# Moving the first half's merged low parts from GpSimd to VectorE, spacing out the second half's gate loads, and one scaling and one store of the last rows

## The chip, the cores and the metric

One core of one Trainium2 chip runs the whole program. The metric is the device time of one execution in microseconds (us); the kernel before takes 1205.59 us (median of 3 runs, 1204.64 to 1205.98). Smaller is better. Engines: TensorE (PE) multiplies matrices, and loads of its weights have a row of their own, PEld; VectorE (DVE), ScalarE (ACT) and GpSimd (POOL) do elementwise work; SyncE (SP) issues nearly all DMAs. Each engine runs its own list of instructions strictly in order; semaphores tie the lists together.

## The reference

1024 tokens of width 1024 with 16 meta tokens ahead of them go through one mixer block, one squared-ReLU MLP and a final RMS norm. The part that matters here is the merge at the end of the mixer:

```python
y_b = jnp.einsum('blc,cd->bld', o.reshape(B, L, GLA_VAL), w_gla_out)
m = jax.nn.sigmoid(ga) * y_a + jax.nn.sigmoid(gb) * y_b
return jnp.einsum('bld,de->ble', m, w_out)
```

`o` is the gated linear attention output (4 heads of 128 values), `y_a` the output of the pooling branch. After the MLP each row is divided by its root mean square and multiplied by `norm_final`.

## The kernel before, in words

**Arithmetic.** Products are float32 of near full precision: every operand is split into a high part (a rounding copy by ScalarE) and a low part (operand minus high part), and TensorE adds three products, high by high, high by low and low by high (`mm3`, L256 to L258). So each intermediate that is multiplied again costs one ScalarE copy and one subtraction, on VectorE or GpSimd.

**The merge.** Tokens are handled in two halves `h` of 512. All tensors are transposed, channels on partitions. The merged tensor `m` has 8 channel blocks `d` of 128 for each half. `yb_block(n, h)` (L1127) makes two of them: TensorE multiplies 256 columns of `w_gla_out` (a high and a low slot of the ring `W1`) by the attention output `yg[h]`, heads k = 0 to 3 in this order, 12 matmuls for each block; VectorE multiplies the PSUM bank by the stored gate sigmoid(gb) (buffer `gl`: L1161 for h = 0, L1150 for h = 1), and adds the stored sigmoid(ga)·y_a (buffer `ml`, L1162); ScalarE makes the high part `th` (L1165); the low part `tl` is then GpSimd's for h = 0, in two instructions of 256 columns (L1169), and VectorE's for h = 1, where it is put off until after the next block's gate product (`pending`, `late()`, L1167). I call the blocks first-half 0 to 7 and second-half 0 to 7.

**Buffers and loads.** Gates and stored products come from DRAM, 256 KB each, issued by SP: `yb_load` (L1086) writes the first half's into `t1` and `o`, the second half's into `t2` and `o2`, each a ring of three buffers. A buffer can be loaded again when its last reader is done: for `gl` that is the low part. `early_gates` (L1104), called after the last attention unit's inner part has been written down, opens `t2` and `o2`, asks for a piece of `w_out`, and asks for the second half's first three pairs at once. It also opens a section in which the instructions of ScalarE and VectorE stand in the order of the code; elsewhere a scheduler orders them. TensorE's are in the order of the code throughout.

**What runs at the same time.** The first half's blocks fill TensorE's gaps in the last attention unit, p = 1 of the second half (`across`, L1339): the chunk states (L1367), the two parts of the output (L1376 and L1386), its norm (L1395 to L1400), a transpose (L1404), and the gating that writes `yg` for heads 2 and 3 (L1413, L1411 on VectorE, high parts L1415 on ScalarE, low parts L1418 on VectorE). L1381 on ScalarE copies one column of the output bank; L1386 on TensorE waits for it. In the same stretch the ring `W1` is refilled: ScalarE makes the high part of a slot (L83), GpSimd the low part in four pieces until the attention is done (`W1.eng = pool`), VectorE after that (L87).

Behind the second half's blocks stands `out_tile`, which multiplies `m` by `w_out`. The split of `w_out` comes in four pieces kk, 256 rows each (L1498 on ScalarE, L1499 on VectorE); pieces 1 to 3 are loaded (L1490) into `acc`, which lies where `t1`, `o` and other buffers of the attention were, so the load of piece 1 waits until the last reader of those is done. SP stands in the order of the code from there on, and the second half's later gate loads are behind that load on SP.

**The end.** The last 4 row tiles t = 0 to 3 (`finish_row` with tail, L1729) leave one after the other: VectorE adds the last product (L1767), ScalarE squares and sums the left half (L1742), the inverse root takes two ScalarE steps (L220, L222) and four small VectorE ones (L221, L224, L228, L229), ScalarE scales the right half (L1745), VectorE the left half (L1746), and SP stores first the right half, then the left half (L1748).

Of the kernel before, what the change touches and what calls it, by code (L numbers as in the profile page):

```python
# [11 lines left out]
ACT = mybir.ActivationFunctionType  # L12
ALU = mybir.AluOpType
AX = mybir.AxisListType

P = 128
# [4 lines left out]
HALF = 512  # L21
# [93 lines left out]
def kernel(  # L115
# [3 lines left out]
    nc = tc.nc  # L119
    x = x[0]  # L120
    out = out[0]
# [4 lines left out]
    act, dve, pool, pe = nc.scalar, nc.vector, nc.gpsimd, nc.tensor  # L126
# [74 lines left out]
    def f32(ap):  # L201
        return ap.bitcast(F32)
# [256 lines left out]
    def nxt(key):  # L459
        i = S["n" + key]  # L460
        S["n" + key] += 1
        return S[key][:, i % S["d" + key]]
# [625 lines left out]
    def yb_load(n, h):  # L1088

        if n >= 8 or (n, h) in staged:  # L1090
            return
        d = 2 * YB[h][n // 2] + n % 2
        gl, ml = staged[n, h] = (nxt("t2"), nxt("o2")) if h else (nxt("t1"), nxt("o"))
        nc.sync.dma_start(gl, gb_dram[d, h])
        nc.sync.dma_start(ml, ma_dram[d, h])
# [10 lines left out]
    def early_gates():  # L1106

        in_order("order", mybir.EngineType.Activation, mybir.EngineType.DVE)
        left.pop_to(S["left_n"])
        for key in ("t2", "o2"):  # L1110
            S[key] = right.push(key, [P, 3, HALF], F32)
            S["n" + key], S["d" + key] = 0, 3
        S["raw3"] = right.push("raw3", [P, D], F32)
        fetch_wo(0, 0, S["raw3"])
        for n in range(3):
            yb_load(n, 1)

    kept, pending = {}, []

    def late():  # L1120

        while pending:
            pending.pop(0)()

    halves_of_half = [slice(k * HALF // 2, (k + 1) * HALF // 2) for k in range(2)]

    def yb_block(n, h):  # L1127
        j = YB[h][n]

        def fn(*wbs):  # L1130
            if h == 0 and n > 1:
                kept[j] = wbs[0]
            wb = wbs[0] if wbs else kept[j]
            hi, lo = (t.rearrange("p (k c) -> p k c", k=4) for t in wb)
            assert h or ("o", 0) in done
            yg = S["yg"][h]
            for e in range(2):
                d, w = 2 * j + e, slice(e * P, (e + 1) * P)
                for m in range(2):
                    yb_load(2 * n + e + m, h)  # L1140
                gl, ml = staged[2 * n + e, h]
                b = bank("mm")
                for k in range(4):
                    mm3(
                        b, 1, lambda i: (hi[:, k, w], lo[:, k, w]),
                        lambda i: (yg[:, 0, k], yg[:, 1, k]), first=k == 0, last=k == 3,
                    )
                    yield 3 * 512 / 2400
                if h:
                    dve.tensor_tensor(gl, b, gl, ALU.mult)  # L1150
                    late()
                    yb_load(2 * n + e + 2, h)
                if e and not wbs:
                    W1.done, W1.kept = W1.done + 1, W1.kept - 1
                    W1.top_up()
                elif e:
                    yield "keep" if j in kept else "free"
                if h and e and n == 1:
                    load_wo(0, 1)()
                if not h:  # L1160
                    dve.tensor_tensor(gl, b, gl, ALU.mult)  # L1161
                dve.tensor_tensor(gl, gl, ml, ALU.add)  # L1162
                th = MH[h][:, d]
                tl = ML[h][:, d]
                act.activation(th, gl, ACT.Copy)  # L1165
                if h:
                    pending.append(lambda tl=tl, gl=gl, th=th: dve.tensor_tensor(tl, gl, f32(th), ALU.subtract))  # L1167
                for c in halves_of_half[: 2 - 2 * h]:
                    pool.tensor_tensor(tl[:, c], gl[:, c], f32(th[:, c]), ALU.subtract)  # L1169

        return fn

# [557 lines left out]
    def finish_row(t, tail):  # L1730

        a, (h0, h1) = S["c"][:, t], halves()
        junk = S["w2"]["12"].rearrange("p i c -> p (i c)")[:, (t % 4) * D : (t % 4 + 1) * D]
        if not tail:
            ss = ln_stat[t % 4]
            act.activation(junk, a, ACT.Square, accum_out=ss)
            rs = inv_sqrt(ss, 1, 1.0 / D)
            dve.scalar_tensor_tensor(junk, a, rs, gB, ALU.mult, ALU.mult)
            nc.sync.dma_start(out[t * P : (t + 1) * P, :], junk)
            return  # L1740
        s0, s1 = tails[t]
        act.activation(junk[:, h0], a[:, h0], ACT.Square, accum_out=s0)  # L1742
        dve.tensor_scalar(s1, s1, 1.0 / D, EPS, ALU.mult, ALU.add)
        rs = inv_sqrt(s0, 1, 1.0 / D, s1)
        act.activation(junk[:, h1], a[:, h1], ACT.Copy, scale=rs)  # L1745
        dve.scalar_tensor_tensor(junk[:, h0], a[:, h0], rs, gB[:, h0], ALU.mult, ALU.mult)  # L1746
        for c in (h1, h0):
            nc.sync.dma_start(out[t * P : (t + 1) * P, c], junk[:, c])  # L1748

    tails = [(tiny(1), tiny(1)) for _ in range(4)]  # L1750

# [126 lines left out]
```

## Time and profile before

| what | us |
|---|---|
| median of 3 runs | 1205.59 |
| the profiled execution | 1206.74 |
| its span, first to last instruction | 1205.0 |
| around the span (1206.74 - 1205.0) | 1.7 |
| PE busy | 1186.7 |
| DVE busy | 874.9 |
| ACT busy | 623.9 |
| POOL busy | 60.2 |

The profile is of one execution. A line of the timeline tells the start, the duration, the engine, the source line, the operation with the names out<-in, and, in brackets, how long the engine had been idle and what ended that. A row "x4" merges four equal instructions and runs from the first one's start to the last one's end. In the names, `t` is a gate buffer (`t1` or `t2`), `o` a buffer of stored products, `th` and `tl` the merged tensor's high and low parts, `mix` the attention's scratch, `raw` a weight as loaded, `w1h` and `w1l` the ring's slots. Granted clock is TensorE's share of full speed; it is 0.998 over this span.

### The profile page before, as it was taken

To read this page: it belongs to the slowest core of one execution; us is meant where nothing else is said; L and a number is where in the kernel's file an instruction comes from. 1 tells how busy PE (TensorE), PEld (TensorE's weight loads), DVE (VectorE), ACT (ScalarE), POOL (GpSimd) and SP (SyncE) were. 2 spreads that over 40 slices of the span, in tenths; PEclk is the share of its full clock that TensorE was granted. 3 is DMA by queue.
4 is the path that set the end of the run, shared out by engine and by line. 5 is a ranking of instruction groups with operands and counts; after the bars stand their busy time and mean duration, and the time that the engine had idled before them with its cause. 6 is when DMAs were issued, how large, how long until landed. Compare 5 with 4: busy or idle time off the path is not lost.

```text
span 1205.0 us, 18370 instructions
## 1 busy us (share of the span) xinstructions
PE 1186.7 (98%) x6794; PEld 992.4 (82%) x6794; DVE 874.9 (73%) x1438; ACT 623.9 (52%) x1119; POOL 60.2 (5%) x98
## 2 busy tenths in 40 slices
PE   7999999999999999999999999999999999999997
PEld 7878888898998887888878888888888888888885
DVE  7997677667567887637886767667675887887685
ACT  7677566755446433315654545455454444445554
POOL 2000000000103235000000000000000000000000
PEclk9999999999999999999999999999999999999999
DMA  9043333445107675922254445444479963333532
GB/s 258 2 114 114 109 103 104 150 120 150 64 20 260 188 252 187 324 74 83 88 181 151 158 134 171 143 164 154 135 263 334 338 224 98 97 97 94 169 97 88
DMA packets 144555, 182.24 MB, mean 151 GB/s; under 512 B 10265, under 2 KB 81713, under 8 KB 143953
## 3 DMA queue, kind: packets, MB, share of 16 engines
q1 hardware_dynamic: 143856, 176.81, 46.0%
q0 software_dynamic: 608, 4.26, 1.0%
q8 instruction: 53, 0.87, 0.3%
q14 instruction: 38, 0.30, 0.1%
HBM read 123.36 MB, written 57.67 MB: 150 GB/s over the span
## 4 chain that ended last, share of the span: by engine, by line
PE 89%; DVE 5%; ACT 2%; DMA 2%; issue 1%; POOL 0%; SPq 0%; DVEq 0%; POOLq 0%; ACTq 0%
PE b_mm L256 10%; PE b_mm L258 10%; PE b_mm L257 10%; PE b_ms L258 10%; PE b_ms L257 10%; PE b_ms L256 10%; PE b_x L257 8%; PE b_x L256 8%; PE b_x L258 8%; PE b_sc L1253 1%; PE b_mx L256 1%; DMA ma_dram<-o 1%; PE b_mx L258 1%; PE b_mx L257 1%; DVE ut L787 1%
## 5 line engine op out<-in xcount | busy, mean ns | idle before, releaser
L256 PE MATMUL b_mm<-th,w1h 128*128 128x512 f32 (+1 forms) x308 | 115.5, 375 | 1.5 <-DVE c L822 1.0
L258 PE MATMUL b_mm<-th,w1l 128*128 128x512 f32 (+1 forms) x308 | 114.2, 371 | 0.0
L257 PE MATMUL b_mm<-tl,w1h 128*128 128x512 f32 (+1 forms) x308 | 114.1, 371 | 0.0
L256 PE MATMUL b_x<-th,w1h 128*128 128x512 f32 (+1 forms) x264 | 100.2, 379 | 0.0
L257 PE MATMUL b_x<-tl,w1h 128*128 128x512 f32 (+1 forms) x264 | 100.1, 379 | 0.0
L258 PE MATMUL b_x<-th,w1l 128*128 128x512 f32 (+1 forms) x264 | 99.7, 378 | 0.0
L274 ACT ACTIVATE w1h<-raw 128x512 fp32r<-128x512 f32 x98 | 60.7, 620 | 28.1 <-PE b_ms L257 13.6
L274 ACT ACTIVATE w1h<-fs 128x512 fp32r<-128x512 f32 x78 | 49.0, 630 | 47.9 <-PE b_ms L257 33.7
L275 DVE TENSOR_TENSOR w1l<-raw,w1h 128x512 fp32r<-128x512 f32 x98 | 67.0, 685 | 8.0 <-ACT w1h L274 8.0
L256 PEld LDWEIGHTS b_mm<-th,w1h 128*128 128x128 f32 x308 | 57.8, 188 | 12.4 <-issue 1.4
L258 PEld LDWEIGHTS b_mm<-th,w1l 128*128 128x128 f32 x308 | 57.8, 188 | 10.1
L257 PEld LDWEIGHTS b_mm<-tl,w1h 128*128 128x128 f32 x308 | 57.9, 188 | 9.6
L275 DVE TENSOR_TENSOR w1l<-fs,w1h 128x512 fp32r<-128x512 f32 x78 | 53.4, 686 | 16.2 <-ACT w1h L274 16.1
L274 ACT ACTIVATE w1h<-bt 128x512 fp32r<-128x512 f32 x44 | 27.8, 632 | 67.1 <-issue 62.7
L258 PEld LDWEIGHTS b_x<-th,w1l 128*128 128x128 f32 x264 | 49.7, 188 | 9.5
L256 PEld LDWEIGHTS b_x<-th,w1h 128*128 128x128 f32 x264 | 49.6, 188 | 9.4
L257 PEld LDWEIGHTS b_x<-tl,w1h 128*128 128x128 f32 x264 | 49.6, 188 | 9.3
L1726 DVE TENSOR_TENSOR bt<-w,w 128x512 f32<-128x512 f32 x80 | 54.7, 684 | 2.0 <-DMA w<-in_w_ff_dram 2.0
L274 ACT ACTIVATE fxh<-bt 128x512 fp32r<-128x512 f32 x36 | 22.8, 632 | 55.7 <-issue 50.1
L274 ACT ACTIVATE w1h<-rawx 128x512 fp32r<-128x512 f32 x44 | 27.5, 628 | 44.8 <-PE b_x L257 18.7
L258 PE MATMUL b_ms<-wo,w1l 128*128 128x512 f32 x128 | 49.9, 390 | 0.0
L256 PE MATMUL b_ms<-wo,w1h 128*128 128x512 f32 x128 | 49.8, 389 | 0.0
(452 smaller groups left out, 3331.8 us busy)
## 6 DMA issues: line engine op xcount, KB each, us to landing
hf_dram<-h SPq DMA_DIRECT2D x112, 256.0 KB, 2.1
raw<-hf_dram SPq DMA_DIRECT2D x112, 256.0 KB, 2.7
w<-in_w_ff_dram SPq DMA_DIRECT2D x64, 256.0 KB, 4.6
raw<-in_w_in_dram SPq DMA_DIRECT2D x22, 512.0 KB, 4.4
raw<-in_w_ff_dram SPq DMA_DIRECT2D x16, 512.0 KB, 4.1
rawx<-in_w_ff_dram SPq DMA_DIRECT2D x16, 512.0 KB, 4.1
rawx<-in_w_in_dram SPq DMA_DIRECT2D x10, 512.0 KB, 4.2
xs<-in_x_dram SPq DMA_DIRECT2D x8, 512.0 KB, 5.6
```

The source lines that it names most:

```text
L256: pe.matmul(ps, ah, bh, start=first and i == 0, stop=False, skip_group_check=more)
L257: pe.matmul(ps, ah, bl, start=False, stop=False, skip_group_check=more)
L258: pe.matmul(ps, al, bh, start=False, stop=last and i == n - 1, skip_group_check=more)
L274: act.activation(hi, a, ACT.Copy)
L275: dve.tensor_tensor(lo, a, f32(hi), ALU.subtract)
L787: dve.tensor_tensor(to_, a_, b_, ALU.subtract)
L1253: pe.matmul(b[to, e, j], kk[r, s], qq[r, s], start=True, stop=True, tile_position=(e * CH, u * CH))
L1726: dve.tensor_tensor(bt, w, S["w2"][q[3:]][:, i], ALU.add if q[2] == "+" else ALU.subtract)
```

## The change

Three edits that do not depend on each other:

- First half: the low part leaves GpSimd's two instructions of 256 columns and becomes one VectorE instruction of 512 columns, right behind the high part in the code. The second half's still waits for the next block.
- `early_gates` asks for one pair of the second half instead of three. The second and third pair are asked for in the first half's `yb_block` of n = 2 and n = 3, in the second of its two blocks.
- Last rows: the scaling of the right half of row tile 2 goes from ScalarE to GpSimd; the right half of row tile 3 is stored by ScalarE instead of SP.

```diff
-        for n in range(3):
-            yb_load(n, 1)
+        yb_load(0, 1)
...
-    halves_of_half = [slice(k * HALF // 2, (k + 1) * HALF // 2) for k in range(2)]
...
                 if h and e and n == 1:
                     load_wo(0, 1)()
+                if e and not h and n > 1:
+                    yb_load(n - 1, 1)
                 if not h:
                     dve.tensor_tensor(gl, b, gl, ALU.mult)
                 dve.tensor_tensor(gl, gl, ml, ALU.add)
                 th = MH[h][:, d]
                 tl = ML[h][:, d]
                 act.activation(th, gl, ACT.Copy)
+                low = lambda tl=tl, gl=gl, th=th: dve.tensor_tensor(tl, gl, f32(th), ALU.subtract)
                 if h:
-                    pending.append(lambda tl=tl, gl=gl, th=th: dve.tensor_tensor(tl, gl, f32(th), ALU.subtract))
-                for c in halves_of_half[: 2 - 2 * h]:
-                    pool.tensor_tensor(tl[:, c], gl[:, c], f32(th[:, c]), ALU.subtract)
+                    pending.append(low)
+                else:
+                    low()
...
-        act.activation(junk[:, h1], a[:, h1], ACT.Copy, scale=rs)
+        if t == 2:
+            pool.tensor_scalar(junk[:, h1], a[:, h1], rs, None, ALU.mult)
+        else:
+            act.activation(junk[:, h1], a[:, h1], ACT.Copy, scale=rs)
         dve.scalar_tensor_tensor(junk[:, h0], a[:, h0], rs, gB[:, h0], ALU.mult, ALU.mult)
-        for c in (h1, h0):
-            nc.sync.dma_start(out[t * P : (t + 1) * P, c], junk[:, c])
+        for q, c in ((act if t == 3 else nc.sync, h1), (nc.sync, h0)):
+            q.dma_start(out[t * P : (t + 1) * P, c], junk[:, c])
```

The lists of instructions that this gives stand against the old ones as follows. TensorE's is the same, instruction for instruction. In the changed kernel the lines of `yb_block` are L1147 (gate product, second half), L1160 (gate product, first half), L1161 (sum), L1164 (high part) and L1165 (low part); `t_2694` is `t1`, `t_4590` is `t2`.

VectorE before, from the first half's blocks 4 and 5 to the first two of the second half; the attention's last gating (L1413, L1411, L1418) stands behind block 5:

```order
L1161 TENSOR_TENSOR t_2694<-b_mm,t_2694 128x512
L1162 TENSOR_TENSOR t_2694<-t_2694,o 128x512
L1413 TENSOR_TENSOR mix<-b_m_4816,mix 128x512
L1411 TENSOR_TENSOR mix<-b_m_4816,mix 128x4x64 x2
L1418 TENSOR_TENSOR yg_3485<-mix,yg_3485 128x512 x2
L1161 TENSOR_TENSOR t_2694<-b_mx,t_2694 128x512
L1162 TENSOR_TENSOR t_2694<-t_2694,o 128x512
L1161 TENSOR_TENSOR t_2694<-b_mm,t_2694 128x512
L1162 TENSOR_TENSOR t_2694<-t_2694,o 128x512
L1150 TENSOR_TENSOR t_4590<-b_mm,t_4590 128x512
```

VectorE now, from block 5's product to the low part of block 6 and, behind the rows shown as "...", that of block 7:

```order
L1160 TENSOR_TENSOR t_2694<-b_mm,t_2694 128x512
L1161 TENSOR_TENSOR t_2694<-t_2694,o 128x512
L1165 TENSOR_TENSOR tl_136<-t_2694,th_132 128x512
L1413 TENSOR_TENSOR mix<-b_m_4808,mix 128x512
L1411 TENSOR_TENSOR mix<-b_m_4808,mix 128x4x64 x2
L1418 TENSOR_TENSOR yg_3485<-mix,yg_3485 128x512 x2
...
L1165 TENSOR_TENSOR tl_136<-t_2694,th_132 128x512
...
L87 TENSOR_TENSOR w1l<-raw_120,w1h 128x1024
L1165 TENSOR_TENSOR tl_136<-t_2694,th_132 128x512
```

Each first-half block has gained a row, L1165, behind its sum: it reads `th`, which ScalarE writes from that sum, and the next block's product stands behind it. The low parts of blocks 3, 4 and 5 now stand ahead of the attention's gating, that of block 7 behind the refill of a `W1` slot (L87).

SyncE (all DMAs), in the stretch where the first half's blocks 2 and 3 ask for their gates; `raw_116` is one of the two buffers in which `w_gla_out` arrives. One piece of the difference:

```order
 L1095 DMA o<-ma_dram 128x512
+L1094 DMA t_4590<-gb_dram 128x512
+L110 DMA raw_116<-in_w_gla_out_dram 128x4x256
+L963 DMA ma_dram<-o 128x512
+L1094 DMA t_2694<-gb_dram 128x512
+L1095 DMA o<-ma_dram 128x512
+L1094 DMA t_2694<-gb_dram 128x512
+L1095 DMA o<-ma_dram 128x512
+L1393 DMA mix<-r_dram 128x2x512
 L1094 DMA t_4590<-gb_dram 128x512 x2
-L963 DMA ma_dram<-o 128x512
-L1094 DMA t_4590<-gb_dram 128x512
```

The weight load of 512 KB now stands ahead of the last store of the pooling branch (L963), two gate loads of the second half behind it.

## The prediction

> **What bounds the kernel now.** I read the page first, engine shares and chain, then the timeline of the stretch that the change touches.
>
> ```profile
> PE 1186.7 (98%) x6794; PEld 992.4 (82%) x6794; DVE 874.9 (73%) x1438; ACT 623.9 (52%) x1119; POOL 60.2 (5%) x98
> PE 89%; DVE 5%; ACT 2%; DMA 2%; issue 1%; POOL 0%; SPq 0%; DVEq 0%; POOLq 0%; ACTq 0%
> ```
>
> TensorE is busy 98% of the span and carries 89% of the chain. Its list of instructions stays the same, so the time moves only where TensorE's waits change, or behind its last product. In the merge the timeline shows two waits:
>
> ```profile
> 455.95 0.45 PE L1386 MATMUL b_m<-W,mix 64*64 64x128 f32 x8 [1.18 <-ACT small L1381]
> 462.92 0.47 PE L256 MATMUL b_mx<-yg,w1h 128*128 128x512 f32 x1 [0.20 <-DVE t L1161]
> ```
>
> Together 1.38 us: all that the two edits of the merge can win. What they can lose is set by VectorE's room there, from the windows (PE, PEld, DVE, ACT, POOL busy):
>
> ```profile
> 469.37:491.10 21.73, 21.73 (x97) 18.02 (x96) 20.69 (x27) 8.22 (x11) 5.80 (x5) 1.00 0.57 180
> ```
>
> In the second half's eight blocks VectorE is busy 20.69 of 21.73 us, beside a TensorE without a gap. Work put on VectorE ahead of this stretch has nowhere to go.
>
> **First wait: L1386.** The chain of waits (start, duration, what) that leads to it:
>
> ```profile
> 444.80 6.78 DMA ma_dram<-o
> 451.64 2.74 DMA o<-ma_dram
> 454.48 0.70 DVE t L1162
> 455.20 0.63 ACT th L1165
> ```
>
> The last store of the pooling branch lands at 451.58, the products of first-half block 2 are loaded into its buffer, the sum and the high part follow, and L1381, behind that high part on ScalarE, lets L1386 go. Now SP has the weight load (512 KB) ahead of that store, and it waits until GpSimd has read its buffer:
>
> ```profile
> 442.37 3.00 POOL L87 TENSOR_TENSOR w1l<-raw,w1h 128x256 fp32r<-128x256 f32 x4 [10.82 <-ACT w1h L83]
> 448.00:450.00 2.00, 2.00 (x11) 1.61 (x10) 1.86 (x6) 0.93 (x1) 1.08 (x3) 1.00 1.02 386
> ```
>
> GpSimd ends at 445.37, so the store is issued near 445.9 instead of 444.80, 1.1 us later, and has 512 KB ahead of it where a 256 KB gate load stood.
> At the 386 GB/s of the second row (last column) 256 KB more are 0.7 us. If both add up, +1.8 us. In the other direction the two gate loads that no longer compete can let it land earlier; then VectorE sets the end: it now has block 1's low part ahead of block 2, which I place at 452.5 to 453.2, so block 2's sum can start at 453.95, 0.5 us before the 454.48 above. The queue is full either way, so issuing later costs little of itself; I take **+0.4 us**, bounds -0.5 and +1.8.
>
> **The low parts' round trips.** Block by block, VectorE before, from block 3 on to the attention's gating (L1413, L1411, L1418):
>
> ```profile
> 462.09 0.68 DVE L1161 TENSOR_TENSOR t<-b_mx,t 128x512 f32<-128x512 f32 x1
> 462.81 1.25 DVE L1162 TENSOR_TENSOR t<-t,o 128x512 f32<-128x512 f32 x1
> 467.15 0.68 DVE L1413 TENSOR_TENSOR mix<-b_m,mix 128x512 f32<-128x512 f32 x1
> 467.75 0.74 DVE L1411 TENSOR_TENSOR mix<-b_m,mix 128x256 f32<-128x256 f32 x2
> 468.53 2.39 DVE L1418 TENSOR_TENSOR yg<-mix,yg 128x512 fp32r<-128x512 f32 x2
> 461.39 3.27 POOL L87 TENSOR_TENSOR w1l<-raw,w1h 128x256 fp32r<-128x256 f32 x4 [4.07 <-ACT w1h L83]
> 464.80 5.57 POOL L1169 TENSOR_TENSOR tl<-t,th 128x256 fp32r<-128x256 f32 x6
> ```
>
> Blocks 3, 4 and 5 take 467.15 - 462.09 = 5.06 us. Now each has its low part behind the sum, it needs ScalarE's high part, and VectorE, strictly in order, waits for that. The second half shows one such trip:
>
> ```profile
> 479.39 0.68 DVE L1162 TENSOR_TENSOR t<-t,o 128x512 f32<-128x512 f32 x1
> 480.11 0.63 ACT L1165 ACTIVATE th<-t 128x512 fp32r<-128x512 f32 x1 [2.00 <-DVE t L1162]
> 480.78 0.69 DVE L1167 TENSOR_TENSOR tl<-t,th 128x512 fp32r<-128x512 f32 x1
> 481.38 0.69 DVE L1162 TENSOR_TENSOR t<-t,o 128x512 f32<-128x512 f32 x1
> ```
>
> From the sum's end (480.07) to the low part's start 0.71, to the next instruction 0.60 (481.38 - 480.78). A block is 0.72 (462.09 to 462.81) + 0.68 + 0.71 + 0.60 = 2.71 us; block 3, whose sum still runs beside GpSimd's refill, has 1.25 for 0.68, 3.28. Three blocks: 8.70, +3.64, so L1413 starts at 470.79. I use 0.68 for the sums of 4 and 5, since GpSimd's 16 halves are gone.
>
> The Trainium skill, "SBUF — State Buffer", section "Who interferes with whom", says that a VectorE instruction with two SBUF inputs and a GpSimd instruction that reads SBUF exclude each other, the second waiting until the first is done. The rows agree: the sum took 1.25 beside GpSimd's refill and 0.68 at 479.39 with GpSimd idle; if the stretch had another cause and stayed, blocks 4 and 5 would be 0.57 longer each, +1.1 us on the sum.
>
> Behind L1413 the gating takes its turns with ScalarE, two high parts in 1.29, the second after L1411: high part of head 2 at 471.51 to 472.14, of head 3 at 472.16 to 472.79; low part of head 2 472.18 to 472.87, of head 3 472.83 to 473.52. TensorE before:
>
> ```profile
> 469.37 0.39 PE L256 MATMUL b_mm<-yg,w1h 128*128 128x512 f32 x1
> 470.95 0.39 PE L257 MATMUL b_mm<-yg,w1h 128*128 128x512 f32 x1
> 472.08 0.39 PE L256 MATMUL b_x<-yg,w1h 128*128 128x512 f32 x1
> ```
>
> The second half's block 0 starts at 469.37, nothing holds it there (first-half block 5's bank is read by 468.8), and at 470.95 it multiplies head 2's low part. That comes at 472.87; TensorE starts 0.15 behind a release (462.77 to 462.92 above): 473.02, a wait of **+2.1 us**. Head 3's follows 0.68 later and is on time. Bounds 1.5 (trips 0.2 shorter each) and 2.6 (GpSimd's refill slows one more).
>
> **SP, behind block 7's low part.** The load of `w_out` piece 1 goes where `t1` lay. It waited for GpSimd's last half; now it waits for block 7's low part on VectorE:
>
> ```profile
> 477.82 0.38 SPq L1490 DMA_DIRECT2D acc<-in_w_out_dram x1
> 478.37 0.35 SPq L1094 DMA_DIRECT2D t<-gb_dram x1
> DMA to landing us min/median/max: 4.3/4.3/4.3
> 482.74 0.69 DVE L1150 TENSOR_TENSOR t<-b_mm,t 128x512 f32<-128x512 f32 x1 [0.67 <-DMA t<-gb_dram]
> 483.95 1.22 DVE L87 TENSOR_TENSOR w1l<-raw,w1h 128x1024 fp32r<-128x1024 f32 x1
> 486.14 0.39 PE L258 MATMUL b_x<-yg,w1l 128*128 128x512 f32 x1
> ```
>
> VectorE's list from head 3's low part (next start 473.43) to block 7's: nine instructions of 512 columns at 0.60, two of 1024 at about 1.13 (1.22 less the overlap of 0.09 that the 0.69 to 0.60 above shows), and 0.3 until second-half block 0 ends on TensorE: 473.43 + 5.40 + 2.26 + 0.3 = 481.4, done 482.1. So this load goes out 4.3 us later, though TensorE is only 2.1 later, and what is queued behind it on SP goes with it: the gate of second-half block 3, 0.55 behind, lands 4.3 after that, 487.0. VectorE already waited 0.67 for it; now its product starts at 487.1, and behind it stand a low part and L87, the low part of the weights of second-half block 6: 488.3 to 489.5. TensorE wants them at 486.14 + 2.1 = 488.2 and gets them at 489.65: **+1.4 us**. Bounds 0 (the gate lands in 2.9) and 2.2.
>
> Last of this kind is `w_out` piece 3:
>
> ```profile
> 493.54 1.22 DVE L1499 TENSOR_TENSOR wo<-acc,wo 128x1024 fp32r<-128x1024 f32 x1
> 495.43 0.39 PE L257 MATMUL b_mm<-wo,th 128*128 128x512 f32 x1
> ```
>
> From 488.3 on stand three more instructions of 1024 columns and nine of 512 ahead of it, 8.8 us: 497.1 to 498.3, with up to 0.5 for a gate. TensorE wants it at 495.43 + 2.1 + 1.4 = 498.9. On time: **0**, at most +0.8. What follows on TensorE moves with it: its list is the same, and its few waits behind it hang on its own results.
>
> **The last rows.** ScalarE's scaling of row 2 stands inside row 3's chain:
>
> ```profile
> 1198.36 0.71 ACT L1745 ACTIVATE w<-c,small 128x512 f32<-128x512 f32 x1
> 1198.97 0.28 ACT L220 ACTIVATE small<-small 128x1 f32<-128x1 f32 x1
> 1200.90 0.33 SPq L1748 DMA_DIRECT2D out_dram<-w  x1
> 1201.35 0.36 SPq L1748 DMA_DIRECT2D out_dram<-w  x1
> DMA to landing us min/median/max: 2.5/2.5/2.5
> 249.46 1.29 POOL L877 TENSOR_TENSOR mw<-raw,mw 128x512 fp32r<-128x512 f32 x1 [9.00 <-DMA gb_dram<-o]
> ```
>
> Without it L220 can start up to 0.61 earlier, less the end of the squaring ahead of it: 0.4. The trace has no GpSimd instruction of this kind; L877 with two inputs takes 1.29, and with one input it should not take longer. It runs beside VectorE's scaling of row 2, and if that stretches by 0.57 (1.25 against 0.68 above), the 0.4 is gone. The last store no longer waits behind its neighbour on SP: 1201.35 - 1200.90 = 0.45. No ScalarE store is in the trace: at best it also lands as the first of a pair does (another 0.4), at worst the new queue costs as much as a slow landing does against the 2.5 here (4.3 - 2.5 = 1.8). I take -0.45 and half of the 0.4: **-0.6 us**, bounds -1.2 and +1.0.
>
> The Trainium skill, "DMA: Bandwidth & Descriptors", section "Issuing engines are not separate DMA queues", says that an issue from another engine saves only the time of the issue, since all share the 16 DMA engines. By that the gain is the 0.45; if the queues were independent, 0.85. No run here shows it yet.
>
> **Sum.** 0.4 + 2.1 + 1.4 + 0 - 0.6 = +3.3 us. On the profiled execution, 1205.0 span and 1.7 around it, 1206.74 + 3.3 = 1210.0; that execution is 1.15 above the median of the runs, so on the median 1205.59 + 3.3 = **1208.9 us**.
>
> **Rivals.**
>
> *The round trip alone.* SP's delay is absorbed, because the gate lands 1.4 us faster into idle DMA queues. For it: nothing else is under way there. Against: the row above had idle queues too, and took 4.3. Sum 0.4 + 2.1 - 0.6 = +1.9: 1207.5.
>
> *The queue ahead of L1386 grows.* The store lands the full 1.8 later. For it: SP's blocked load; against: the full DMA queue. Sum 1.8 + 2.1 + 1.4 - 0.6 = +4.7: 1210.3.
>
> *VectorE is free in time.* The other side: the gating keeps its place, both waits go, and the tail wins. The gating is on time if the three blocks take at most 8.70 - 2.1 = 6.6 us, 0.7 less for each, which is just the wait for ScalarE; this would need the scheduler's order not to hold on VectorE. For it: GpSimd's reads did stretch VectorE, the pair L1418 took 2.39 where two times 0.68 would do. Against: I have already counted that, and the low part stands behind the sum in the list. Sum -1.38 - 0.6 = -2.0: 1203.6.
>
> **How the numbers follow.** The forecast 0.58, its own range 1208.0 to 1209.9; the round trip alone 0.20; the longer queue 0.14; the free VectorE 0.08. About 0.2% (2.4 us) is what a measurement of this kernel can tell from no change. Slower: 0.58 + 0.14, less 0.02 for forecasts that end below 1208.0: 0.70. Within: 0.20 + 0.02 + 0.05 of the free VectorE: 0.27. Faster: 0.03, since even -2.0 falls short. The range goes from 1206.8 (the round trip alone with the lower bound 1.5 of the trips) to 1211.2 (the longer queue with 0.9 more from refill or tail).
>
> **What would show it.** Right: TensorE waits about 2 us at L257 of second-half block 0 for VectorE's L1418, and over 1 us at an L258 near 489 for L87; L1490 goes out near 482; L1386 waits 1 to 2 us; the last store is issued before 1201 plus the delay so far. Wrong: no wait at L1418 (the round trips are not paid), L1490 near 478 (block 7's low part is early), or a new wait behind 500, which I have taken for none.

## The result, and the profile after

| what | before | changed |
|---|---|---|
| median (6 executions each, taken side by side), us | 1205.78 (1204.64 to 1207.00) | 1212.39 (1211.98 to 1213.17) |
| ratio to before | | 1.0056, 95% interval 1.0045 to 1.0067 |
| the profiled execution, us | 1206.74 | 1212.29 |
| its span, us | 1205.0 | 1210.5 |
| end of TensorE's last product, us | 1196.97 | 1201.52 |
| from there to the end of the span, us | 7.99 | 9.00 |

The changed kernel is 6.6 us slower; 3.3 were forecast, and 1211.2 was the end of the range. Of the 5.5 us between the two profiled spans, 4.55 lie ahead of TensorE's last product and 1.0 behind it. Another 1.0 is the choice of the execution: the profiled one of before lies 0.96 above its median, the changed one 0.10 below.

In the page after, the shares (first row) and the chain (second row) read nearly as before; TensorE's waits are too short to show there.

```profile
PE 1189.9 (98%) x6794; PEld 994.6 (82%) x6794; DVE 876.6 (72%) x1446; ACT 623.3 (51%) x1118; POOL 48.1 (4%) x83
PE 87%; DVE 6%; ACT 2%; DMA 2%; issue 1%; POOL 0%; SPq 0%; DVEq 0%; POOLq 0%; ACTq 0%
```

VectorE has eight instructions more and only 1.7 us more of busy time: GpSimd's halves no longer stretch what VectorE does beside them (the pair L1418 takes 1.36 now instead of 2.39). What was lost is in TensorE's row of the timeline:

```profile
457.17 0.45 PE L1386 MATMUL b_m<-W,mix 64*64 64x128 f32 x8 [2.31 <-ACT small L1381]
473.84 0.50 PE L257 MATMUL b_mm<-yg,w1h 128*128 128x512 f32 x1 [0.23 <-DVE yg L1418]
490.40 0.50 PE L258 MATMUL b_x<-yg,w1l 128*128 128x512 f32 x1 [1.07 <-DVE w1l L87]
```

Three waits, at the three places that the prediction named. The first is 1.13 longer than the 1.18 of before. The second seems tiny, but a row's bracket shows only what the modelled end of the product ahead leaves over: against before, this start has moved from 470.95 to 473.84, by 2.89. So I pair TensorE's rows with those of before and read how late each one is: 1.2 us at L1386, 2.8 at 462, 2.3 at 465, 3.0 at 475, 4.4 at 487, 4.8 at 500, 4.6 at the end.

Between 457 and 462 TensorE became 1.6 us later with no wait at all (0.5 of it is regained by 465, where the kernel before waited itself). The window there (the column behind POOL is the granted clock) and rows behind L1386:

```profile
457.10:461.40 4.30, 4.23 (x40) 3.38 (x41) 2.19 (x4) 1.70 (x5) 0.00 (x0) 0.62 0.99 357
458.80 0.63 PE L257 MATMUL b_mm<-yg,w1h 128*128 128x512 f32 x1
459.23 0.63 PE L258 MATMUL b_mm<-yg,w1l 128*128 128x512 f32 x1
461.69 0.39 PE L258 MATMUL b_mm<-yg,w1l 128*128 128x512 f32 x1
461.92 0.40 PE L256 MATMUL b_mm<-yg,w1h 128*128 128x512 f32 x1
```

The clock was granted at 0.62 in this window: 0.50 from 458.15 to 461.56 and full around that, so that it fell 1.0 us after the long wait had ended. Product follows product by 0.43 us (458.80 to 459.23) instead of 0.23 (461.69 to 461.92). I had not thought of this. The Trainium skill, "TensorE: Matmul & The Clock Gate", section "Part 1: The HAM clock gate", gives 426.7 and 215.7 ns for 512 columns at half and full clock, and the rows agree with the first and lie some 0.01 us above the second.

The chain of waits shows that this is not what set the second wait. It runs from the store through L1386 and the attention's norm into the low parts' round trips on VectorE and ScalarE, and TensorE's slow products are not in it:

```profile
446.41 5.50 DMA ma_dram<-o
451.98 3.64 DMA o<-ma_dram
455.71 0.70 DVE t L1161
456.43 0.63 ACT th L1164
457.17 1.15 PE b_m L1386 x32
...
469.72 0.70 DVE t L1161
470.44 0.64 ACT th L1164
471.14 0.57 issue
471.71 0.69 DVE mix L1413
472.43 0.64 ACT yg L1415
473.10 0.70 DVE yg L1418
473.84 0.50 PE b_mm L257
```

The end of the program, in the timeline (L1746 is GpSimd's scaling, L1749 VectorE's, L1751 the stores):

```profile
1202.80 0.75 DVE L1749 SCALAR_TENSOR_TENSOR w<-c,small,gB 128x512 f32<-128x512 f32 x1
1203.02 1.98 POOL L1746 TENSOR_SCALAR w<-c,small 128x512 f32<-128x512 f32 x1 [737.44 <-ACT w L1742]
1204.53 0.75 DVE L1749 SCALAR_TENSOR_TENSOR w<-c,small,gB 128x512 f32<-128x512 f32 x1
1205.03 0.33 SPq L1751 DMA_DIRECT2D out_dram<-w  x1
1205.28 0.37 ACTq L1751 DMA_DIRECT2D out_dram<-w  x1
1205.45 0.88 SPq L1751 DMA_DIRECT2D out_dram<-w  x2
```

GpSimd needs 1.98 us for row 2's right half and ends at 1205.00; the store of it on SP goes out at 1205.03. Row 2's left half, ready since 1203.55 (the first L1749), and row 3's left half, ready at 1205.28 (the second), stand behind it (the row x2). So two stores of row 2 that used to be long gone are now in front of the last one.

### The profile page after: what moved, and what is told of

Read it like the earlier page. It is cut to its first block, busy times and chain, and to the rows that moved or that the text cites. A ratio compares the mean times of both kernels' runs of the same rounds, so it can differ in the third digit from the quotient of the medians.

```text
span 1210.5 us, 18366 instructions
## 1 busy us (share of the span) xinstructions
PE 1189.9 (98%) x6794; PEld 994.6 (82%) x6794; DVE 876.6 (72%) x1446; ACT 623.3 (51%) x1118; POOL 48.1 (4%) x83
## 4 chain that ended last, share of the span: by engine, by line
PE 87%; DVE 6%; ACT 2%; DMA 2%; issue 1%; POOL 0%; SPq 0%; DVEq 0%; POOLq 0%; ACTq 0%
PE b_mm L256 10%; PE b_mm L258 10%; PE b_mm L257 10%; PE b_ms L257 9%; PE b_ms L258 9%; PE b_ms L256 9%; PE b_x L257 8%; PE b_x L256 8%; PE b_x L258 8%; PE b_sc L1253 1%; PE b_mx L256 1%; PE b_mx L258 1%; PE b_mx L257 1%; DMA t<-gb_dram 1%; DVE w1l L275 1%
## 5 line engine op out<-in xcount | busy, mean ns | idle before, releaser
L256 PE MATMUL b_mm<-th,w1h 128*128 128x512 f32 (+1 forms) x308 | 115.5, 375 | 1.3 <-DVE c L822 1.0
L258 PE MATMUL b_mm<-th,w1l 128*128 128x512 f32 (+1 forms) x308 | 114.2, 371 | 0.0
L257 PE MATMUL b_mm<-tl,w1h 128*128 128x512 f32 (+1 forms) x308 | 114.2, 371 | 0.0
L256 PE MATMUL b_x<-th,w1h 128*128 128x512 f32 (+1 forms) x264 | 100.2, 380 | 0.0
L257 PE MATMUL b_x<-tl,w1h 128*128 128x512 f32 (+1 forms) x264 | 100.2, 379 | 0.0
L258 PE MATMUL b_x<-th,w1l 128*128 128x512 f32 (+1 forms) x264 | 99.8, 378 | 0.0
L256 PEld LDWEIGHTS b_mm<-th,w1h 128*128 128x128 f32 x308 | 57.8, 188 | 12.2 <-issue 2.1
L258 PEld LDWEIGHTS b_mm<-th,w1l 128*128 128x128 f32 x308 | 57.9, 188 | 10.1
L257 PEld LDWEIGHTS b_mm<-tl,w1h 128*128 128x128 f32 x308 | 57.9, 188 | 9.5
L258 PEld LDWEIGHTS b_x<-th,w1l 128*128 128x128 f32 x264 | 49.7, 188 | 9.6
L256 PEld LDWEIGHTS b_x<-th,w1h 128*128 128x128 f32 x264 | 49.6, 188 | 9.4
L257 PEld LDWEIGHTS b_x<-tl,w1h 128*128 128x128 f32 x264 | 49.6, 188 | 9.2
L258 PE MATMUL b_ms<-wo,w1l 128*128 128x512 f32 x128 | 49.9, 390 | 0.0
L256 PE MATMUL b_ms<-wo,w1h 128*128 128x512 f32 x128 | 49.8, 389 | 0.0
```

The lines of the kernel that those rows point to most:

```text
L256: pe.matmul(ps, ah, bh, start=first and i == 0, stop=False, skip_group_check=more)
L257: pe.matmul(ps, ah, bl, start=False, stop=False, skip_group_check=more)
L258: pe.matmul(ps, al, bh, start=False, stop=last and i == n - 1, skip_group_check=more)
```

## The experiments

Theory: three losses. The spaced gate loads let the weight load of 512 KB get ahead of the pooling branch's last store on SP, which makes L1386 late; the low parts' round trips and SP's blocked queue cost what the prediction says; in the last rows GpSimd's scaling is slow and SP's order passes it on. Rivals: the tail is a gain and the merge has lost it all; or the halved clock is the missing piece of the merge.

Executions of one kernel differ by some 3 us here, so small differences are read from the traces, and medians carry the larger ones. All kernels side by side; the numbers without a unit are us. "L1386" is its start, with its wait. "Steps" are how much later TensorE becomes, against the profile of before, at three places: second-half block 0 (L256 and L257), L258 of second-half block 6 with L87, and the first L257 with `w_out` (piece 3, L1499). "Tail" is from the end of TensorE's last product to the end of the span. A dash: no wait in the trace.

| kernel | L1386 | steps | tail | ratio to before |
|---|---|---|---|---|
| before | 455.95, 1.18 | 0, 0, 0 | 7.99 | 1 |
| changed | 457.17, 2.31 | 0.7, 1.35, 0.4 | 9.00 | 1.0056 (1.0045 to 1.0067) |
| e1_tail_both | 454.95, - | 0, 0, 0 | 8.99 | 1.0006 (0.9997 to 1.0015) |
| e2_tail_store | 454.97, 0.41 | 0, 0, 0 | 8.20 | 1.0007 (0.9998 to 1.0016) |
| e3_tail_scale | 454.84, - | 0, 0, 0 | 8.66 | 1.0005 (0.9997 to 1.0014) |
| e11_scale_tt | 454.85, 0.41 | 0, 0, 0 | 8.58 | 1.0007 (0.9998 to 1.0016) |
| e12_row2_last | 455.47, 0.94 | 0, 0, 0 | 8.58 | 1.0006 (0.9997 to 1.0015) |
| e4_merge_only | 456.24, 1.28 | 1.8, 1.5, 0.4 | 8.00 | 1.0044 (1.0032 to 1.0057) |
| e5_gates_only | 455.97, 1.38 | 0, 0, 0 | 7.75 | 1.0012 (1.0003 to 1.0020) |
| e6_lows_only | 455.35, 0.40 | 1.8, 1.5, 1.0 | 8.04 | 1.0038 (1.0025 to 1.0050) |
| e7_warm | 456.96, - | 1.8, 1.7, 1.1 | 7.86 | 1.0049 (1.0037 to 1.0062) |
| e8_lows_late | 456.35, 1.75 | 1.9, 1.1, 0.2 | 7.95 | 1.0039 (1.0025 to 1.0052) |
| e9_ma_store_act | 455.16, 0.41 | 1.8, 1.6, 0.3 | 7.76 | 1.0033 (1.0021 to 1.0046) |
| e10_wo1_pool | 455.51, 0.53 | 1.8, 0, 0.9 | 8.10 | 1.0030 (1.0019 to 1.0042) |

One interval sorts the merge: from L1386 to the L257 of second-half block 0 that reads L1418's result, TensorE takes 15.0 in the seven kernels with GpSimd's low parts, and 16.65 to 16.67 in the six in which VectorE waits for ScalarE at each low part, the changed kernel with its halved clock among them (e8_lows_late: 16.7).

Of the executions' differences, two sources show in these profiles: L1386's wait, and a wait near 889 for L1664 on VectorE, far behind the merge, which was between 0 and 1.5 in kernels with and without the change.

### The last rows

Both edits of the last rows alone, on the kernel before:

```diff
-        act.activation(junk[:, h1], a[:, h1], ACT.Copy, scale=rs)
+        if t == 2:
+            pool.tensor_scalar(junk[:, h1], a[:, h1], rs, None, ALU.mult)
+        else:
+            act.activation(junk[:, h1], a[:, h1], ACT.Copy, scale=rs)
...
-        for c in (h1, h0):
-            nc.sync.dma_start(out[t * P : (t + 1) * P, c], junk[:, c])
+        for q, c in ((act if t == 3 else nc.sync, h1), (nc.sync, h0)):
+            q.dma_start(out[t * P : (t + 1) * P, c], junk[:, c])
```

> The kernel before with only the two edits of the last rows. Theory (GpSimd's scaling of row 2 is slow, 1.98 us in the changed kernel, and SP, in order, holds row 3's left half behind it): +0.9 us, between +0.6 and +1.3; SP issues row 3's left half 4.4 us behind TensorE's last product or a little later, with row 2's two stores right ahead of it. Rival (the prediction's term, with the loss of the changed kernel lying in the merge alone): -0.6 us.

The tail is 8.99, as in the changed kernel; the eight kernels with the old last rows have 7.75 to 8.10, mean 7.93. So +1.0, and no gain. The medians (+0.5) cannot tell it from nothing. In e1's timeline, and its list of DMA issues for row 3's left half (last column: us to landing):

```profile
1199.22 1.89 POOL L1746 TENSOR_SCALAR w<-c,small 128x512 f32<-128x512 f32 x1 [722.79 <-ACT w L1742]
1202.05 0.40 SPq L1751 DMA_DIRECT2D out_dram<-w  x1
out_dram<-w SPq DMA_DIRECT2D x1, 256.0 KB, 3.2
```

The last store goes out 4.40 us behind TensorE's last product (1197.65), before 4.38: what ScalarE's store saves, the queue behind GpSimd takes. It lands in 3.17 instead of 2.50, with four stores under way, and from the last landing to the end of the span (the closing, from here on) it is 1.43 instead of 1.11. These three make up the 1.0.

Only ScalarE's store:

```diff
-        for c in (h1, h0):
-            nc.sync.dma_start(out[t * P : (t + 1) * P, c], junk[:, c])
+        for q, c in ((act if t == 3 else nc.sync, h1), (nc.sync, h0)):
+            q.dma_start(out[t * P : (t + 1) * P, c], junk[:, c])
```

> The kernel before with only the ScalarE store of row 3's right half. Theory (the store itself is a gain, the scaling on GpSimd loses it): -0.4 us, the left half issued by SP without a neighbour ahead of it. Rival (the store from another engine is the loss, a new queue lands late): +0.5 us or more, its landing above 3 us.

Neither. The two stores go out together:

```profile
1200.78 0.39 ACTq L1748 DMA_DIRECT2D out_dram<-w  x1
1200.81 0.33 SPq L1748 DMA_DIRECT2D out_dram<-w  x1
out_dram<-w ACTq DMA_DIRECT2D x1, 256.0 KB, 2.8
out_dram<-w SPq DMA_DIRECT2D x1, 256.0 KB, 2.5
```

The last issue is 3.96 behind TensorE's last product, 0.42 earlier than before. But the landings are 2.5 and 2.8 now instead of 2.1 and 2.5, so the last one comes 6.71 behind it instead of 6.88, and the closing is 1.49 instead of 1.11. Net +0.2 for a gain of 0.42 in issuing. The Trainium skill, "DMA: Bandwidth & Descriptors", section "Issuing engines are not separate DMA queues", lets only the time of the issue be saved; here 0.17 of the 0.42 are left at the last landing, and nothing at the end of the span.

Only GpSimd's scaling:

```diff
-        act.activation(junk[:, h1], a[:, h1], ACT.Copy, scale=rs)
+        if t == 2:
+            pool.tensor_scalar(junk[:, h1], a[:, h1], rs, None, ALU.mult)
+        else:
+            act.activation(junk[:, h1], a[:, h1], ACT.Copy, scale=rs)
```

> The kernel before with only row 2's right half scaled on GpSimd; row 3 keeps both stores on SP. Theory: all four last stores queue on SP behind GpSimd, row 3's left half as the fourth: +1.2 us, between +0.8 and +1.6. Rival (the prediction's reading, a scaling of at most 1.29 us that is hidden and frees ScalarE): -0.2 us.

The tail is 8.66, +0.7: the theory's direction, a little below its range. The last store goes out 4.92 behind the last product, 0.52 later than in e1, and lands at the same point, 7.56 behind it against 7.57. In both, four stores leave from 3.50 on, so this points to the four together, and not to who issues the last, as what sets that landing. With the old closing (1.10) the whole 0.7 is GpSimd's scaling and what queues behind it.

GpSimd's scaling as a product of two tensors, with both edits:

```diff
-            pool.tensor_scalar(junk[:, h1], a[:, h1], rs, None, ALU.mult)
+            pool.tensor_tensor(junk[:, h1], a[:, h1], rs.broadcast_to([P, HALF]), ALU.mult)
```

> Both edits of the last rows on the kernel before, GpSimd's scaling written as a product of two tensors (the scale broadcast along the row) instead of a tensor and a scalar per partition. Theory A (the kind of instruction is slow on GpSimd: 1.9 us against the 1.29 us of a product of two tensors elsewhere): it takes 1.3 us, row 2's store goes out 0.6 us earlier, from TensorE's last product to the end 8.4 us instead of 9.0. Theory B (VectorE's work beside it makes it slow): it takes 1.8 us or more again, 9.0 us.

```profile
1198.46 1.38 POOL L1746 TENSOR_TENSOR w<-c,small 128x512 f32<-128x512 f32 x1 [722.12 <-ACT w L1742]
1199.17 0.69 DVE L224 SCALAR_TENSOR_TENSOR small<-small 128x1 f32<-128x1 f32 x1
```

Theory A: 1.38 instead of 1.89, with VectorE's L1749 beside it in both. Yet the tail only falls to 8.58: L224, a step of row 3's own chain with one value per partition, now takes 0.69, against 0.22 in the trace of before and 0.33 in e1. It ends at 1199.86, GpSimd's product at 1199.84.

Row 2's right half stored behind row 3's left half:

```diff
         for q, c in ((act if t == 3 else nc.sync, h1), (nc.sync, h0)):
-            q.dma_start(out[t * P : (t + 1) * P, c], junk[:, c])
+            if (t, c) != (2, h1): left = q.dma_start(out[t * P : (t + 1) * P, c], junk[:, c])
+        if t == 3:
+            with tc.issue_after(left.ins): nc.sync.dma_start(out[2 * P : 3 * P, h1], S["w2"]["12"].rearrange("p i c -> p (i c)")[:, 2 * D + HALF : 3 * D])
```

> Both edits of the last rows on the kernel before, but SP issues row 2's right half (GpSimd's) behind row 3's left half. Theory (GpSimd's late half holds the stores behind it on SP): row 3's left half goes out 3.8 us behind TensorE's last product instead of 4.4, row 2's right half at 4.2, the end 8.2 us behind the last product instead of 9.0. Rival (four stores within a microsecond land late in whatever order, as the one that took 3.17 us to land): the last landing takes over 3 us again and the end stays at 8.9 us or more.

```profile
1200.24 0.33 SPq L1751 DMA_DIRECT2D out_dram<-w  x1
1200.66 0.38 SPq L1753 DMA_DIRECT2D out_dram<-w  x1
```

The issues come where the theory has them, 3.79 and 4.21 behind the last product: GpSimd's half did hold the stores behind it. But the last one takes 2.95 to land, and the tail is 8.58, between the two expectations. So SP's order is 0.4 of the 1.0. The rest is a later landing (2.95 against 2.50 before) and a longer closing (1.42 against 1.11); what causes those two is not shown.

### The merge

The changed kernel with the old last rows (the diff of e1 taken back):

> The changed kernel with its last rows as before. Theory (the merge costs what TensorE's last product shows, 4.55 us): +4.6 us, and with the tail edits alone it adds up to the whole. Rival (the two stages act on each other, or the stretch that is lost in the merge comes back later): clearly less than +4 us, so that the two parts do not add up.

+5.5 in the median, interval 3.9 to 6.9; TensorE's last product ends 5.52 later, 1.5 of it at the wait near 889. Merge and tail add up within what the runs can tell (5.5 and 1.0 against 6.6). In this execution L1386 waited 1.28 and the clock stayed full, so it shows the prediction's chains without the drop. VectorE's timeline:

```profile
470.77 0.68 DVE L1413 TENSOR_TENSOR mix<-b_m,mix 128x512 f32<-128x512 f32 x1
487.11 0.69 DVE L1147 TENSOR_TENSOR t<-b_mm,t 128x512 f32<-128x512 f32 x1 [2.39 <-DMA t<-gb_dram]
488.32 1.22 DVE L87 TENSOR_TENSOR w1l<-raw,w1h 128x1024 fp32r<-128x1024 f32 x1
```

and SP's and TensorE's:

```profile
482.20 0.38 SPq L1490 DMA_DIRECT2D acc<-in_w_out_dram  x1
472.17 0.50 PE L256 MATMUL b_mm<-yg,w1h 128*128 128x512 f32 x1 [0.99 <-ACT yg L1415]
472.90 0.50 PE L257 MATMUL b_mm<-yg,w1h 128*128 128x512 f32 x1 [0.23 <-DVE yg L1418]
489.59 0.50 PE L258 MATMUL b_x<-yg,w1l 128*128 128x512 f32 x1 [1.22 <-DVE w1l L87]
```

L1413 was predicted at 470.79, the L257 at 473.02, L1490 at 482.1, the gate product at 487.1, L87 at 488.3 and TensorE behind it at 489.65. That the first two are met so closely is partly luck: those instants left L1386 at 455.95, here it came 0.30 later, and block 3's sum took 0.93 where 1.25 was counted. The one surprise is that TensorE waits one product earlier as well, for the high part of head 2.

Only the spaced gate loads (the low parts back on GpSimd):

```diff
                 else:
-                    low()
+                    for c in (slice(0, 256), slice(256, 512)): pool.tensor_tensor(tl[:, c], gl[:, c], f32(th[:, c]), ALU.subtract)
```

> Second-half gates asked for one by one, low parts of the first half still on GpSimd, last rows as before. Theory (the weight load that is now ahead of the pooling branch's last store on SP makes L1386 late, and the wait of over 2 us halves TensorE's clock): L1386 waits 2.2 us or more, the twelve products behind it run at about half the clock for 3 us, no wait at L1418, in all +2.4 us. Rival (the prediction's term: the store's delay is mostly absorbed by the full DMA queue, and what made L1386 late is block 1's low part on VectorE): +0.4 us, a wait of 1.2 to 1.6 us and no drop of the clock.

The median is +1.3, between the two. The profile shows the wait of 1.38 and a full clock, as the rival has it, with none of the low parts that the rival makes responsible. But two of the eleven executions took 1210.80 and 1210.07 at a mean granted clock of 0.995 and 0.996; the other nine took 1205.80 to 1207.77 at 0.998 or 0.999. In e8, below, it is one of five (1212.68 at 0.996, the others up to 1210.41 at 0.998). So the mean clock was lower in some executions only, and those are 2.3 to 3.7 us longer than the middle one of the others. They have no trace; that it is the drop behind L1386, and how much of the time is a longer wait ahead of it, is argued, not shown. In the changed kernel the clock makes no such difference: 1211.98 to 1212.49 at 0.997, 1212.95 and 1213.17 at 0.998.

Only the low parts (the gate loads at once):

```diff
-        yb_load(0, 1)
+        for n in range(3): yb_load(n, 1)
```

> Low parts of the first half on VectorE, second-half gates asked for at once as before, last rows as before. Theory: L1386 waits 1.2 us as before, no drop of the clock there, TensorE waits about 2 us at L257 of second-half block 0 for L1418 and about 1.2 us at L258 for L87, in all +3.2 us. Rival (VectorE's extra low part ahead of block 2 is what made L1386 late): L1386 waits 2 us or more and the total is as with both edits of the merge, +4.6 us.

L1386 waits 0.40, as in the kernels with GpSimd's low parts: VectorE's low part ahead of block 2 does not make it late. The first two steps, 1.8 and 1.5, are near the theory's 2 and 1.2. The total, +4.6, is the one that the rival named, but not by the rival's way: piece 3 of `w_out` adds 1.0, which the theory left out.

```profile
499.02 0.50 PE L257 MATMUL b_mm<-wo,th 128*128 128x512 f32 x1 [0.69 <-DVE wo L1499]
```

TensorE kept busy ahead of L1386 by ten extra products that nothing reads:

```diff
         act.activation(seen, o[:, :, 3, P - 1], ACT.Copy)
+        if (p, half) == (1, 1):
+            spare, yg = bank("ms"), S["yg"][0]
+            for _ in range(10):
+                pe.matmul(spare, yg[:, 0, 0, :P], yg[:, 0, 0], start=True, stop=True)
```

> Both edits of the merge, last rows as before, and ten extra products of 512 columns (yg by yg, into a spare bank, never read) ahead of the six products in front of L1386, which fill TensorE's wait. Theory (the halved clock costs 1.5 us of TensorE's time, but VectorE's round trips set the start of L257 of second-half block 0, so it is hidden there): no drop of the clock behind L1386, TensorE's wait at L257 for L1418 grows from 0.6 to about 2 us, the total the same as without the extra products within 0.3 us. Rival (the halved clock is a cost of its own): 1.3 to 1.5 us faster than without them.

1212.07, 5.8 above before, against 5.5 of e4: no gain, as the theory has it. The pair is weak evidence, though: the trace of e4 had no drop to cure, and in e7 the extra products themselves may have held L1386, which starts without a wait right behind them. The stronger evidence is the changed kernel's own profile. It had the drop, and its first step is 0.7 where the five others with these round trips, at full clock, have 1.8: the trips had covered 1.1 of the 1.6 us. From L1386 to that L257 it took 16.67 at half clock, and 16.65 or 16.66 in those five. TensorE would have waited for L1418 anyway.

Low parts put off, as the second half's are:

```diff
                 else:
-                    low()
+                    pending.append(low)
...
                 if not h:
-                    dve.tensor_tensor(gl, b, gl, ALU.mult)
+                    dve.tensor_tensor(gl, b, gl, ALU.mult); late()
```

> Both edits of the merge, last rows as before, but the first half's low parts are put off until behind the next block's gate product, as the second half's are. Theory (the wait for ScalarE goes, 8.4 us for three blocks become 5.7; but the late L1386 and the halved clock now set TensorE alone): no wait at L1418, TensorE is 2.4 us late there instead of 2.9, block 7's low part comes earlier and L87 waits 0.5 us or less, in all +2.8 us. Rival (the round trips cost their full 2.1 us and go with the wait): +1.5 us or less.

Both are wrong on the step: 1.9, with the round trips gone. VectorE's timeline has the reason:

```profile
466.59 0.69 DVE L1161 TENSOR_TENSOR t<-t,o 128x512 f32<-128x512 f32 x1
469.16 0.69 DVE L1160 TENSOR_TENSOR t<-b_mm,t 128x512 f32<-128x512 f32 x1 [1.88 <-DMA t<-gb_dram]
```

A gate's buffer comes free with its low part. Put off by a block, the low part lets the load start a block later (issued at 465.24, on SP behind a weight load at 464.76; in e4 at 456.88), and block 5's product waits 1.88 us for its gate: the wait for ScalarE has become a wait for a DMA. The median is 4.2 above before, e4's 5.5; up to 500 the traces differ by 0.3, and the wait near 889 was 1.2 in e4 and none here, so little of a gain can be read from this pair.

The pooling branch's last store issued by ScalarE:

```diff
-                nc.sync.dma_start(ma_dram[2 * j + e, h], o)
+                (act if (j, e, h) == (3, 1, 1) else nc.sync).dma_start(ma_dram[2 * j + e, h], o)
```

> Both edits of the merge, last rows as before, and the last store of the pooling branch issued by ScalarE, so that it is not behind the weight load on SP. Theory (with the gate loads spaced out, that weight load waits for GpSimd ahead of the store, and this makes L1386 1.1 us later than with the loads at once): the store goes out near 445, L1386 waits 0.6 us or less, the whole stretch behind it moves with it, since VectorE's gating hangs on it: 1.0 us faster than both edits alone, +4.3 us on the kernel before. Rival (the store's place decides nothing, the other loads that share the DMA queue then do): L1386 waits 1.2 us or more, no change.

```profile
443.91 0.35 ACTq L963 DMA_DIRECT2D ma_dram<-o  x1
455.16 0.45 PE L1386 MATMUL b_m<-W,mix 64*64 64x128 f32 x8 [0.41 <-ACT small L1381]
```

The theory: the store goes out ahead of the weight load (445.82 on SP), L1386 starts at 455.16, 1.1 ahead of e4, and the median is 3.7 above before instead of 5.5; of that gain of 1.8 the traces show 1.1 at L1386. With the loads at once the store went out at 443.72 to 444.80 in seven profiles (mean 444.11) and L1386 started at 455.20 on average; with the loads spaced out and the store on SP, at 446.14 to 446.54 (446.35) and 456.25, in five (e7, with its extra products there, left out). So 2.24 us of delay at the issue are 1.28 at the landing (449.95 and 451.23 on average) and 1.05 at L1386.

Piece 1 of `w_out` loaded by GpSimd's queue (the expectation's "L499" is L1499):

```diff
-            nc.sync.dma_start(at.rearrange("p (k c) -> p k c", k=2), ap)
+            (pool if kk == 1 else nc.sync).dma_start(at.rearrange("p (k c) -> p k c", k=2), ap)
```

> Both edits of the merge, last rows as before, and piece 1 of w_out loaded from GpSimd's queue instead of SP's, so that it still waits for block 7's low part but nothing on SP waits behind it. Theory (the prediction's chain: SP held by that load, the gate of second-half block 3 behind it, VectorE waits for the gate, L87 behind that is late for L258): the gate is issued near 478.5 instead of 482.6, VectorE's wait of 2.4 us for it goes, no wait at L258 of second-half block 6, at least 1.3 us faster than both edits alone. Rival (VectorE simply has too much to do there, the gate's lateness covers nothing else): TensorE's 1.5 us come back at L258 or at L499's place behind it, at L257 of the first product with w_out, and the total changes by less than 0.5 us.

```profile
479.69 0.32 SPq L1094 DMA_DIRECT2D t<-gb_dram  x1
485.65 1.23 DVE L87 TENSOR_TENSOR w1l<-raw,w1h 128x1024 fp32r<-128x1024 f32 x1 [0.26 <-ACT w1h L83]
497.52 0.50 PE L257 MATMUL b_mm<-wo,th 128*128 128x512 f32 x1 [0.57 <-DVE wo L1499]
```

The gate goes out 3 us earlier, L87 starts at 485.65 instead of 488.32, and the wait at L258 is gone: the chain was SP's queue. But 0.9 comes back at L1499 (0.4 in e4), so the net is about 1.0 of the 1.5, between the theory and the rival. The median is 3.6 above before instead of 5.5; an L1386 that was 0.7 earlier has its share in that.

None of these versions beats the kernel before.

## Why the prediction was wrong, point by point

**First wait, +0.4.** Too small, in the right place. It is +1.13 in the two profiles and +1.05 between the averages of seven and five. The step that failed is the reading of one trace as if every execution were like it. The trace of before had the store go out at 444.80, the latest of seven (mean 444.11). It also had GpSimd end its refill at 445.37, because the last of its four pieces took 0.74; in each of the other thirteen profiles that piece took 1.19 or 1.20. So the store goes out at 446.35 on average, not 445.9, and the delay of the issue is 2.24, not 1.1. And "issuing later costs little of itself" is wrong by the 1.05, which e9 takes back. VectorE's extra low part ahead of block 2 does not show at L1386 (e6). And I took the run median as 1.15 below that execution without asking which wait made it slow; L1386, 0.75 above the mean of the seven, is one.

**The low parts' round trips, +2.1.** Right in place and cause, 0.3 too large: 1.8 in five of the six kernels that have them. From L1386 to the L257 the prediction has 17.07 (473.02 - 455.95), those kernels 16.65 to 16.67, mostly because block 3's sum was shorter than counted. That e4 met the instants to 0.12 us is luck to that extent, since its late L1386 made up for it. In the changed kernel's own profile they add 0.7, because the halved clock had made TensorE late already; its loss and the trips do not add, since the trips hang on L1386 and not on TensorE's pace. At 475 the changed kernel is 3.0 late, against 0.4 + 2.1 = 2.5.

**SP behind block 7's low part, +1.4.** Right: 1.35 in the changed kernel, 1.5 in e4, with the queue as the cause (e10).

**`w_out` piece 3, 0.** 0.4 in the changed kernel and 1.0 and 1.1 in e6 and e7; the bound was 0.8. The working had left a margin of 0.6 us (498.3 against 498.9), less than the counts and the gate loads ahead of it vary: over the six kernels with the round trips and e8 this wait is 0.2 to 1.1. Which of the two sets it in each was not tried.

**The last rows, -0.6.** The sign was wrong; it is +1.0, and with 1.6 it is the largest single miss. Two steps failed. The first is "with one input it should not take longer": GpSimd's scaling took 1.98, not 1.29. I did not walk SP's queue behind it either, where row 2's two halves now stand in front of row 3's left half; so the 0.45 for the neighbour was not won, as a new neighbour came. This edit alone costs 0.7 (e3). The second is that the term counts issues and takes the last landing and the closing as fixed. ScalarE's store alone goes out 0.42 earlier, and the span ends 0.2 later (e2). With both edits the last store goes out as late as before, lands in 3.17 instead of 2.50, and the closing is 1.43 instead of 1.11 (e1): that is the +1.0. A GpSimd scaling of 1.38 did not save the term: the tail was still 8.58, with L224 stretched and the same late landing and longer closing (e11). L220 did start without the scaling ahead of it, and the chain from the last product to the last scaling fell from 3.19 to 3.01 us; nothing of that reached the end. The stretch of L1746 on VectorE, which I feared, did not come (0.75 as before), but L224 on VectorE took 0.34 instead of 0.22.

**Sum.** In the profiled executions 4.55 and 1.0 against 3.9 and -0.6. The last 1.0 of the 6.6 is the choice of the execution (see the result). The rivals: at L1386 the runs lie between the forecast's +0.4 and the longer queue's +1.8, and the tail is on the other side of both; the free VectorE did not happen. The forecast's sign was right all the same, slower by more than 0.2%.

## What to carry to other kernels

An instruction that is taken off one engine's chain has to be followed into the queue of whatever takes its result: here the chain through ScalarE became 0.2 us shorter, and the stores behind GpSimd's late result made the end 0.7 us later (e3). A duration that only one execution shows (a DMA landing in 6.78 us under a full queue) is one draw; ask which wait would swing with it before building a term on it. And waits that hang on one another are not added: follow the chain from the last one back.

## What the runs showed of the hardware

- TensorE's clock fell to half in the changed kernel's profile, from 458.15 to 461.56 (3.41 us), 1.0 us after a wait of 2.31 us had ended (0.43 instead of 0.23 us for each product of 512 columns). It stayed full behind waits of 1.28, 1.38 and 1.75, one profile each. In all fourteen profiles it also fell 2.2 to 5.3 us behind TensorE's last product. The Trainium skill, "TensorE: Matmul & The Clock Gate", section "Part 1: The HAM clock gate", has it fall after at least one idle window of about 3.4 us that runs freely. The varying delay behind the last product agrees with a window that runs freely. The length does not agree: the wait of 2.31 us and eight of those fourteen delays (2.2 to 3.3 us) are shorter. Whether the 32 small products of L1386, between the wait and the drop, count as idle was not tried.
- Of a VectorE sum of two tensors in SBUF and a piece of GpSimd's refill beside it, the one that started second was stretched. In the trace of before GpSimd started first (444.63, then VectorE at 444.80): 0.74 for GpSimd, 1.11 for VectorE. In the other thirteen VectorE started first: 0.69 or 0.70 for VectorE, 1.19 or 1.20 for GpSimd.
- A step on one value per partition was stretched too: L224 on VectorE took 0.69 us beside GpSimd's product of two tensors and ended 0.02 us behind it (e11). It took 0.33 or 0.34 beside GpSimd's tensor-by-scalar scaling, and 0.22 with GpSimd idle.
- A GpSimd tensor-by-scalar instruction on 128x512 took 1.89 to 1.98 us where a product of two tensors of that size took 1.38 in the same place. Why is open.
- With one of the last stores issued by ScalarE the span ends 1.42 to 1.50 us behind the last landing, without it 1.10 to 1.15 (the eight kernels with the old last rows, and e3). Why is open; it is about as much as the store's earlier issue saves.
